# Strassen's seven quarter products for the output projection of a hybrid gMLP and attention layer

## The chip, the cores and the metric

The kernel runs on one core of a Trainium2 chip. The metric is the device time of one execution in microseconds (us), the median of the runs of one program. TensorE is written PE, VectorE DVE, ScalarE ACT, GpSimd POOL; SP is the queue that issues most DMAs.

## What is computed

One layer of a diffusion trunk with 1024 latent tokens and 128 context tokens of width 1024, all in 32-bit floats. A gMLP group and an attention group of four heads each give 512 columns per token; they are gated, put side by side and projected:

```python
def _back(x, gate, a_out, attn, g_b, w_o):
    y = jnp.concatenate([a_out, attn * jax.nn.silu(g_b)], axis=-1) @ w_o
    return x + gate * y
...
y_prompt = _rmsnorm(xp, final_g)
y_sample = _rmsnorm(xs, final_g)
```

`w_o` is 1024 x 1024. The change touches this product and what follows it.

## The kernel before

Tokens are cut into nine tiles of 128: tiles 0 to 7 are latent, tile 8 is context. After the input projections the gated gMLP output stands in `mixA`, the attention output in `mixB`, both 128 x 4 x 1152: four chunks of 128 mix columns, then tokens. So `mixA` is the upper half of the projection's inner dimension (chunks k = 0 to 3), `mixB` the lower (k = 4 to 7).

A product of 32-bit accuracy is made of three passes. Each operand is split into a high part of type float32r and a low part, operand minus high part (`lo_of`, L111, on DVE); the passes are high x high, high x low, low x high (`out_terms`, L1793).

The order on every engine is written out by hand: from L1774 on, `manual_schedule` keeps the instructions of PE, ACT, DVE and POOL in the order in which Python records them, and SP's queue is ordered as well. Python keeps a clock of its own (`now`): `run` (L207) records a step and moves the clock by its cost, `later(dt, fn)` (L167) records `fn` when the clock passes now + dt, `merged` (L212) interleaves two lists of steps. An instruction that must wait therefore holds up all that was recorded behind it on its engine.

The attention goes through 32 heads (8 tiles x 4). Scores, maximum (L1478), exponentials (L1488), the scaling of the 128 x 1280 exponentials by POOL (`divide`, L1491), then transposes on PE (L1550), the split of the transposed values into `ph` (ACT, L1554) and `pl` (DVE, L112), and the products with the values (L1574 to L1576), two heads at a time. `closed` and `opened` end and begin pools of SBUF; a tile of a new pool waits for the last users of what lay there.

Beside it, from head 11 on, the rows of `w_o` are loaded (`wo_piece`, L1630) and split by `split_job` (L1608): high part by POOL, low part by DVE, one job after each `divide`. `his` and `los` are the lists of such jobs; `wo_need` (L1660) records what is missing before a matmul uses it. The split pieces of `w_o` fill the SBUF areas that the attention no longer uses (`flat`, and the key tiles `kch`, `kcl`, `krh`, `krl`). Tiles 8 and 0 are split in the same way; 20 of their steps are interleaved with the last heads (`early`, L1840).

After the last head the rest follows tile by tile: 8 and 0, then 1 to 7 (L1916 to L1935). A tile takes 2 halves x 8 chunks x 3 passes = 48 matmuls of 512 columns; the last one has its second half in two quarters (`LASTP`). Splits of the next tile: two ACT copies and two DVE low parts. `finish` (L1865) multiplies a half out of PSUM by the gate, adds the residual row `xr`, lets ACT square it with a running sum, and then scales the row by the inverse root (Newton's steps on DVE) and the norm's weight `fg`. `finish_last` (L1881) does the same for tile 7 in a shorter chain, with POOL preparing the weighted row `z` and the store cut over two queues.

The gates come from DRAM (`gdram`), spread over all partitions.

Of the kernel before, what the change touches and what calls it, by code (L numbers as in the profile page):

```python
# [14 lines left out]
ALU = mybir.AluOpType  # L15
# [79 lines left out]
def tile_hymba_step(ctx: ExitStack, tc: tile.TileContext, I, O):  # L95
# [156 lines left out]
    gdram = gd.tile([4, 512], F32, tag="gdram", name="gdram")  # L252
    scl = pc.tile([P, NT], F32, tag="scl", name="scl")
# [1211 lines left out]
    es = {}  # L1465
    s2 = pss.tile([P, 2, 256], F32, tag="s2", name="s2", bufs=1)

    def softmax(t, h, lat_, con_):
# [305 lines left out]
    with tc.manual_schedule(engines=engines):  # L1774
# [3 lines left out]
        def mix_tiles(t):  # L1778
            mh[t] = flat[0][4 + len(mh) % 2].rearrange("p (c q) -> p c q", c=8)
            ml[t] = wo.tile([P, 8, P], F32R, tag="ml", name=f"ml{t}", bufs=2)  # L1780
            sl = slice(t * P, (t + 1) * P)
            return [(mh[t][:, 4 * i : 4 * i + 4, :], ml[t][:, 4 * i : 4 * i + 4, :], src[:, :, sl]) for i, src in enumerate((mixA, mixB))]

        def mix_split(t):
            for hi, lo, src in mix_tiles(t):
                S.copy(hi, src)
                lo_of(lo, src, hi)

        def mix_jobs(t):
            for i, (hi, lo, src) in enumerate(mix_tiles(t)):  # L1790
                split_job(lambda hi=hi, src=src: pool_copy(hi, src), lambda hi=hi, lo=lo, src=src: lo_of(lo, src, hi), ("m", t, i))
# [12 lines left out]
        for c in range(len(pairs)):  # L1804
# [11 lines left out]
            if 2 * c + LEAD + 1 == 11:  # L1816
                closed(c_ra)
                c_wo, wo = opened("wo", side="left")
                for k in range(2):
                    wo_piece(k, *flat[0][2 * k : 2 * k + 2])  # L1820
                mix_jobs(8)
                mix_jobs(0)
# [10 lines left out]
        for t in (8, 0):  # L1833
            wps[t] = [psw.tile([P, 512], F32, tag="w", name=f"w{t}{i}") for i in range(2)]

        def load_xr(t):
# [3 lines left out]
        early = [  # L1840
            (0.65, lambda t=t, i=i, k=k: out_terms(t, wps[t][i], 512 * i, 512 * i + 512, [k]))
            for k in range(5) for t in (8, 0) for i in range(2)
        ]
# [10 lines left out]
    for t in (8, 0, 1, 2):  # L1854
        load_xr(t)
# [3 lines left out]
    gate = {}  # L1859

    for cond in (1, 0):
        gate[cond] = ep.tile([P, 4, 256], F32, tag=f"gate{cond}", name=f"gate{cond}")
        nc.sync.dma_start(gate[cond], gdram.rearrange("j (c r) -> c j r", c=2)[cond : cond + 1].broadcast_to([P, 4, 256]))

    def finish(t, parts):  # L1865
        y = ep.tile([P, 1024], F32, tag="y", name=f"y{t}", bufs=2)
        gt = gate[0 if t < NS else 1].rearrange("p j r -> p (j r)")
        n = len(parts)
        ss = sm.tile([P, 4], F32, tag="fss", name=f"fss{t}")
        for j, (ps, c0, c1) in enumerate(parts):  # L1870
            V.tensor_tensor(y[:, c0:c1], ps, gt[:, c0:c1], op=ALU.mult)
            V.tensor_tensor(y[:, c0:c1], y[:, c0:c1], xr[t][:, c0:c1], op=ALU.add)
            S.activation(xr[t][:, c0:c1], y[:, c0:c1], AF.Square, accum_out=ss[:, j : j + 1])
        s1 = sm.tile([P, 1], F32, tag="fs1", name=f"fs1{t}")
        V.tensor_reduce(s1, ss[:, :n], axis=AX.X, op=ALU.add)
        v = mean_eps(sm, s1, 1, 1024.0, "f")
        r = rsqrt(sm, v, 1, "f")
        V.scalar_tensor_tensor(y, y, r, fg, op0=ALU.mult, op1=ALU.mult)
        nc.sync.dma_start(O["y"][t], y)

    def finish_last(t, parts):  # L1881

        y = ep.tile([P, 1024], F32, tag="y", name=f"y{t}", bufs=2)
        z = ep.tile([P, 1024], F32, tag="xr", name=f"z{t}", bufs=4)
        gt = gate[0].rearrange("p j r -> p (j r)")
        ss = sm.tile([P, 4], F32, tag="fss", name=f"fss{t}")
# [3 lines left out]
        n = len(parts)  # L1890
        for j, (ps, c0, c1) in enumerate(parts):
            V.tensor_tensor(y[:, c0:c1], ps, gt[:, c0:c1], op=ALU.mult)
            V.tensor_tensor(y[:, c0:c1], y[:, c0:c1], xr[t][:, c0:c1], op=ALU.add)
            if j < n - 1:
                S.activation(xr[t][:, c0:c1], y[:, c0:c1], AF.Square, accum_out=ss[:, j : j + 1])
            else:
                V.scalar_tensor_tensor(junk[:, : c1 - c0], y[:, c0:c1], 1.0, y[:, c0:c1], op0=ALU.mult, op1=ALU.mult, accum_out=ss[:, j : j + 1])
            G.tensor_tensor(z[:, c0:c1], y[:, c0:c1], fg[:, c0:c1], op=ALU.mult)
            if j == n - 2:
                V.tensor_reduce(v0, ss[:, : n - 1], axis=AX.X, op=ALU.add)  # L1900
                V.tensor_scalar(v0, v0, 1.0 / 1024.0, EPS, op0=ALU.mult, op1=ALU.add)
# [128 lines left out]
```

## Time and profile before

| | |
|---|---|
| Runs, us | 621.58, 621.84, 623.27; median 621.84 |
| Span of the profiled execution, first to last instruction | 620.5 us (its time as a run is not listed) |
| Mean granted PE clock | 0.991 |
| After the last attention matmul (528.4 to 613.0) | 396 matmuls |
| HBM read and written in the whole execution | 40.87 MB and 4.83 MB |

The span begins with the first instruction of any engine and ends with the last; a run's time has some start and end around it. Busy time of PE says how long matmuls were in flight, and these overlap; PEld is the loading of weights into the array. The chain of waits follows the last instruction back to what released it, step by step. In a group's line stand: source line, engine, operation, tiles written and read with their shapes, count, then busy time in us and mean ns of one, then the idle time of the engine just before and what ended it. In a timeline line: start, length, engine, line, operation; "x2" means that two were merged into one line.

### The profile page before, as it was taken

The page shows a single profiled execution, that of the slowest core. Times are in us where ns is not written, and L with a number is a line of the kernel's source. Part 1 is how long each engine was busy: PE and PEld are TensorE (multiplying, and loading weights), DVE is VectorE, ACT ScalarE, POOL GpSimd, SP SyncE. Part 2 cuts the span into 40 slices and gives each one's busy share as a digit, 9 for nine tenths or more (in the row PEclk, how much of TensorE's full clock was granted, in tenths as well). Part 3 has the DMA queues.
Part 4 walks back from the last instruction along what each step waited for, and adds up shares of the span by engine and source line. Part 5 has one row for each costly group of instructions (what it writes and reads, how often), then busy time and mean ns, then how long its engine had stood idle before and what let it go on. Part 6 is the DMA issues. An engine that isn't in the chain of part 4 may idle for free.

```text
span 620.5 us, 9955 instructions
## 1 busy us (share of the span) xinstructions
PE 606.8 (98%) x3719; PEld 549.0 (88%) x3719; DVE 411.3 (66%) x938; ACT 298.9 (48%) x694; POOL 123.2 (20%) x167
## 2 busy tenths in 40 slices
PE   7999999999999999999999999999999999999995
PEld 6777889999989999999998899999999988888884
DVE  4685457997756468566778656767666754577655
ACT  6556764345433245455675565555555632232212
POOL 2461112000000000433364112323222241000001
PEclk8999999999999999999999999999999999999998
DMA  8992010100351133100010000000101113423311
GB/s 316 393 380 71 0 35 2 35 0 3 134 208 70 64 106 122 38 1 1 1 42 1 1 2 0 2 9 27 35 1 35 35 68 129 144 101 137 115 55 68
DMA packets 15327, 46.32 MB, mean 75 GB/s; under 512 B 1824, under 2 KB 4784, under 8 KB 14768
## 3 DMA queue, kind: packets, MB, share of 16 engines
q1 hardware_dynamic: 15136, 45.50, 20.7%
q8 instruction: 29, 0.48, 0.3%
q10 hardware_dynamic: 144, 0.20, 0.1%
q14 instruction: 18, 0.15, 0.1%
HBM read 40.87 MB, written 4.83 MB: 74 GB/s over the span
## 4 chain that ended last, share of the span: by engine, by line
PE 93%; DVE 3%; DMA 1%; ACT 1%; issue 1%; SPq 0%; ACTq 0%
PE p L953 10%; PE tp L751 8%; PE tp L975 5%; PE pT L1550 5%; PE w L1797 5%; PE w L1799 5%; PE w L1798 5%; PE s L1505 3%; PE s L1506 3%; PE s L1504 3%; PE s L1503 3%; PE o L1574 3%; PE s L1507 3%; PE o L1576 3%; PE o L1575 3%; PE zacc L1389 2%
## 5 line engine op out<-in xcount | busy, mean ns | idle before, releaser
L112 DVE TENSOR_TENSOR pl<-pT,ph 128x512 fp32r<-128x512 f32 x81 | 55.4, 687 | 48.8 <-ACT ph L1554 48.2
L1488 ACT ACTIVATE e<-s,nb,scl 128x256 f32<-128x256 f32 x64 | 56.1, 881 | 35.1 <-DVE nb L1482 35.1
L1494 POOL TENSOR_SCALAR e<-e,rs 128x1280 f32<-128x1280 f32 x32 | 43.0, 1343 | 130.2 <-DVE rs L1493 124.7
L1554 ACT CAST ph<-pT 128x512 fp32r<-128x512 f32 x80 | 45.5, 588 | 41.9 <-PE pT L1550 39.0
L751 PE MATMUL tp<-area,w 128*128 128x384 f32 x288 | 52.5, 338 | 0.0
L751 PEld LDWEIGHTS tp<-area,w 128*128 128x128 f32 x288 | 50.4, 188 | 0.4
L1550 PE MATMUL pT<-ident,e 128*128 128x128 f32 x320 | 48.0, 272 | 1.3 <-DVE pl L112 1.2
L1574 PE MATMUL o<-ph,vh 128*128 128x256 f32 x160 | 47.8, 299 | 0.0
L1576 PE MATMUL o<-ph,vl 128*128 128x256 f32 x160 | 44.9, 281 | 0.0
L1575 PE MATMUL o<-pl,vh 128*128 128x256 f32 x160 | 44.7, 280 | 0.0
L1799 PE MATMUL w<-area,ml 128*128 128x512 f32 (+1 forms) x114 | 43.2, 379 | 0.0
L1550 PEld LDWEIGHTS pT<-ident,e 128*128 128x128 f32 x320 | 37.4, 140 | 4.8 <-issue 1.6
L1478 DVE TENSOR_REDUCE m<-s 128x1 f32<-128x1024 f32 x32 | 38.9, 1217 | 1.5 <-PE s L1507 1.5
L1503 PE MATMUL s<-kch,area 128*128 128x512 f32 (+2 forms) x100 | 38.9, 389 | 0.0
L1236 POOL TENSOR_TENSOR kr<-z,rope 128x64 f32<-128x64 f32 x8 | 2.6, 321 | 172.0 <-ACT z L1245 172.0
L1506 PE MATMUL s<-krh,area 128*128 128x512 f32 (+2 forms) x100 | 35.4, 354 | 0.0
L1505 PE MATMUL s<-kch,area 128*128 128x512 f32 (+2 forms) x100 | 35.4, 354 | 0.0
L1504 PE MATMUL s<-kcl,area 128*128 128x512 f32 (+2 forms) x100 | 35.3, 353 | 0.0
L1507 PE MATMUL s<-krl,area 128*128 128x512 f32 (+2 forms) x100 | 35.1, 351 | 0.0
L975 PE MATMUL tp<-area,w 128*128 128x384 f32 x192 | 35.0, 337 | 0.0
L975 PEld LDWEIGHTS tp<-area,w 128*128 128x128 f32 x192 | 33.6, 188 | 0.4 <-issue 0.4
L1574 PEld LDWEIGHTS o<-ph,vh 128*128 128x128 f32 x160 | 30.1, 188 | 1.6
(375 smaller groups left out, 1601.1 us busy)
## 6 DMA issues: line engine op xcount, KB each, us to landing
ada<-in_ada_ss SPq DMA_DIRECT2D x16, 512.0 KB, 8.1
w2r<-in_w_t SPq DMA_DIRECT2D x12, 512.0 KB, 4.4
x<-in_x SPq DMA_DIRECT2D x9, 512.0 KB, 7.4
xr<-in_x SPq DMA_DIRECT2D x9, 512.0 KB, 4.0
adag<-in_ada_g SPq DMA_DIRECT2D x4, 1024.0 KB, 4.8
wor<-in_w_o SPq DMA_DIRECT2D x8, 512.0 KB, 3.4
out_y<-y SPq DMA_DIRECT2D x8, 512.0 KB, 4.8
wvr<-in_w_v SPq DMA_DIRECT2D x8, 256.0 KB, 9.2
```

What stands on the lines that cost most here:

```text
L112: V.tensor_tensor(lo, src, f32(hi), op=ALU.subtract)
L751: T.matmul(tps[i, g][:, :GW], w_[i][:, k, :], x_[k, g], start=k == 0 and j == 0, stop=k == NK - 1 and j == 2)
L953: T.matmul(banks[key], a_, b_, start=k == 0 and m == 0, stop=k == 3 and m == len(passes) - 1)
L975: T.matmul(tps[c, 2][:, :GW], w_[c][:, k, :], x_[k, 2], start=k == 0 and m == 0, stop=k == NK - 1 and m == 2)
L1488: S.activation(e[:, sl], src, AF.Exp, bias=nb, scale=scl[:, t : t + 1], accum_out=su[:, i : i + 1])
L1503: T.matmul(ps, qh_, kch[:, sl], start=True, stop=False)
L1505: T.matmul(ps, ql_, kch[:, sl], start=False, stop=False)
L1550: T.transpose(ps[:, w : w + P], es[t, h][:, c * P : (c + 1) * P], ident)
L1574: T.matmul(o, vh[:, kt, :], ph[:, sl], start=c == 0, stop=False)
L1575: T.matmul(o, vh[:, kt, :], pl[:, sl], start=False, stop=False)
L1576: T.matmul(o, vl[:, kt, :], ph[:, sl], start=False, stop=c == n - 1)
L1799: T.matmul(ps, b, woh[k][:, c0:c1], start=False, stop=k == NK - 1)
```

## The change

Tiles 0 to 7 are taken in four pairs (a, b). The four quarters of the left side are A11 = `mixA` of a, A12 = `mixB` of a, A21 = `mixA` of b, A22 = `mixB` of b; those of `w_o` are B11, B12, B21, B22 (rows 0 to 511 or 512 to 1023, columns 0 to 511 or 512 to 1023). With

S1 = A21 + A22, S2 = S1 - A11, S3 = A11 - A21, S4 = A12 - S2, T1 = B12 - B11, T2 = B22 - T1, T3 = B22 - B12, T4 = B21 - T2,

seven products of 128 x 512 by 512 x 512 (12 matmuls each: 4 chunks x 3 passes) stand in place of eight: A11 B11, A12 B21, S4 B22, S2 T2, S1 T1, S3 T3, A22 T4. Tile 8 keeps the plain product.

- **Weight sums.** After head 5 a pool `tp` is open. In eight units (chunk k, half of the columns) SP loads four 128 x 256 blocks of `w_o`, POOL makes the four sums, ACT the high parts, DVE the low parts, and SP stores both in DRAM (`tdram`). A unit starts after a `divide`, once per head. Loading and splitting `w_o` itself begins at head 15 instead of 11, with up to two jobs after a `divide`.
- **Fetching them.** Near the end of the attention POOL's queue fetches T2 (4 DMAs) and T3 (8), after it T1 and T4 (8), 4 MB in all of T1 and T4. The gates and the rows of x follow on SP's queue.
- **Block sums** S1 to S4: four POOL operations per pair, made one pair ahead.
- **Splits of the left blocks** into a ring of five buffers, four products ahead (`split`): ACT writes the high part and a copy of the block in PSUM, DVE takes the low part from there.
- **Sums of the products.** K (in A11's place), W (A12's), C (S2's) collect them: DVE adds out of PSUM, POOL multiplies by the gate and adds to the residual row. ACT squares into a buffer that is free. The inverse root is one ACT root with one Newton step.
- **The last pair** has the order A11, A12, S2, S1, S4, S3, A22, and its last product is made and finished in two quarters of 256 columns.

The core of the diff:

```diff
-            spare_hi(1)
-            spare_lo(1)
+            spare_hi(2 if len(his) > 2 else 1)
+            spare_lo(2 if len(los) > 2 else 1)
+            if units and units[0] in traw:
+                unit_of[0](units.pop(0))
...
+        def t_unit(u):
+            k, c = divmod(u, 2)
+            raw = traw[u]
+            b11, b12, b21, b22 = (raw[:, i, :] for i in range(4))
+            sub(G, b11, b12, b11)
+            sub(G, b12, b22, b12)
+            sub(G, b22, b22, b11)
+            sub(G, b21, b21, b22)
+            hi = tp.tile([P, 4, 256], F32R, tag="hi", name=f"thi{u}")
...
+            for i in range(2):
+                later(3.2 + 1.5 * i, lambda i=i: high(i))
+                later(4.0 + 1.5 * i, lambda i=i: low(i))
...
+        def t_piece(m, k, piece):
+            th[m, k], tl[m, k] = piece[:, 0:512], piece[:, 512:1024]
+            G.dma_start(piece, tdram[m - 1, k].rearrange("p s c -> p (s c)"))
...
+        def product(q, ps, c0=0, c1=512, ks=range(4)):
...
+            need(("blk", q))
+            blk = ring(q)
+            for k in ks:
+                bh, bl = right(queue[q][2], k)
+                three(ps[:, c0:c1], (blk[:, 0, k, :], blk[:, 1, k, :]), (bh[:, c0:c1], bl[:, c0:c1]), k == 0, k == 3)
...
+    for n, (m, k) in enumerate([(1, k) for k in range(4)] + [(4, k) for k in range(4)]):
+        t_piece(m, k, tpiece[n])
+        if n == 3:
+            load_gate(0, tag="gate0")
+    load_gate(1, tag="xr", bufs=4)
+    load_xr(8)
+    load_xr(0)
+    load_xr(1)
...
+        def high():
+            cell["raw"] = pso.tile([P, 512], F32, tag="o", name=f"raw{q}").rearrange("p (k c) -> p k c", k=4)
+            S.copy(ring(q)[:, 0], block(n, name))
+            S.copy(cell["raw"], block(n, name))
...
+        def low():
+            lo_of(ring(q)[:, 1], cell["raw"], ring(q)[:, 0])
+            made.add(("blk", q))
...
+            if name == "A11":
+                later(dt, lambda: S.copy(K, view(ps)))
+            elif name == "A12":
+                later(dt, lambda: add(V, view(ps), view(ps), K))
+                later(dt + 0.7, lambda: V.tensor_tensor(C, view(ps), gL, op=ALU.mult))
+                plus(C, a, L, dt + 1.4, 0)
+            elif name == "S2":
+                later(dt, lambda: add(V, K, view(ps), K))
...
+            elif name == "S4" and last:
+                later(dt, lambda: add(V, view(ps), view(ps), W))
+                in_place(a, R, ps, dt + 0.05, 1)
+                gated_add(W, gR, b, R, dt + 0.1)
+                norm(a, dt + 2.0)
...
+                else:
+                    later(dt, lambda: V.tensor_tensor(W, view(ps), gR, op=ALU.mult))
+                    later(dt + 0.2, lambda: V.tensor_tensor(half(b, R), half(b, R), W, op=ALU.add))
+                    later(dt + 0.4, lambda: V.tensor_tensor(ps, ps, gate[0][:, L], op=ALU.mult))
+                    later(dt + 0.6, lambda: V.tensor_tensor(xr[b][:, L], ps, xr[b][:, L], op=ALU.add))
...
+    spare_hi(len(his))
+    for i, c in enumerate((L, R)):
+        in_place(8, c, wps[8][i], 6.5 + 1.4 * i, i)
+    norm(8, 12.0)
+    for n in range(3):
+        pair(n)
+    zl = ep.tile([P, 1024], F32, tag="xr", name="zl", bufs=4)
+    pair(3)
```

`in_place(t, c, ps, ...)` is gate product and residual sum on DVE and the square on ACT, as before but with the product left in PSUM. `norm` is the scaling of a whole row. `finish_last` keeps its chain, with two parts instead of three.

More of the change, by code (lines that the diff above doesn't have):

```diff
@@ L1776, in tile_hymba_step @@
         tail = []
[L1778 to L1787, printed above, removed]
@@ new lines, in need_lo, with t_load @@
+        def need_lo(key):
+            while key not in made:
+                if los:
+                    spare_lo(1)
+                else:
+                    now_, (due, fn) = now[0], waiting.pop(0)
+                    now[0] = due
+                    fn()
+                    now[0] = now_
+        th, tl = {}, {}
+        def t_load(u):
+            k, c = divmod(u, 2)
+            raw = traw[u] = tp.tile([P, 4, 256], F32, tag="raw", name=f"traw{u}", bufs=2)
+            for i, row in enumerate((k, k + 4)):
+                nc.sync.dma_start(raw[:, 2 * i : 2 * i + 2, :], I["w_o"][row].rearrange("p (s c) -> p s c", s=2)[:, :, 256 * c : 256 * c + 256])
@@ L1865, in finish @@
[L1865 to L1886, printed above, removed]
+    ssq = {}
+    def square_of(t, j, junk, c0, c1):
+        if t not in ssq:
+            ssq[t] = sm.tile([P, 4], F32, tag="fss", name=f"fss{t}", bufs=3)
+        S.activation(junk, xr[t][:, c0:c1], AF.Square, accum_out=ssq[t][:, j : j + 1])
@@ new lines, in split @@
+    def split(q, dt):
+        if q >= len(queue):
+            return
+        n, name, _ = queue[q]
+        cell = {}
+        def high():
[5 more added lines that the diff above has]
+            made.add(("blk", q))
+        later(dt, high)
+        later(dt + 1.3, low)
```

296 lines of the change are left out of this document (247 added, 49 removed).

## The prediction

> **What bounds the kernel now.** I read the page first (busy time, then the chain that ended last), then the windows of the stages which the change touches, then the matmuls one by one. The page says that TensorE (PE) is busy nearly all the time and carries the chain.
>
> ```profile
> span 620.5 us, 9955 instructions
> PE 606.8 (98%) x3719; PEld 549.0 (88%) x3719; DVE 411.3 (66%) x938; ACT 298.9 (48%) x694; POOL 123.2 (20%) x167
> ...
> PE 93%; DVE 3%; DMA 1%; ACT 1%; issue 1%; SPq 0%; ACTq 0%
> ```
>
> The windows say the same of both stages, and how much room the others have. Columns: length, then busy time (count) of PE, PE's weight loads, DVE, ACT, POOL, then clock, DMA share, GB/s.
>
> ```profile
> 528.40:613.00 84.60, 84.60 (x396) 70.86 (x395) 55.31 (x149) 20.92 (x49) 2.04 (x2) 1.00 0.30 104
> 360.00:366.00 6.00, 6.00 (x45) 5.56 (x44) 4.63 (x10) 3.39 (x7) 2.56 (x2) 1.00 0.00 0
> 366.00:372.00 6.00, 6.00 (x45) 5.53 (x43) 3.01 (x8) 3.40 (x7) 0.12 (x1) 1.00 0.02 4
> 528.00:532.00 4.00, 4.00 (x21) 3.33 (x20) 0.42 (x1) 0.00 (x0) 0.00 (x0) 1.00 0.93 308
> 36.00:40.00 4.00, 4.00 (x33) 2.88 (x33) 3.86 (x9) 0.35 (x3) 2.36 (x3) 1.00 1.02 400
> ```
>
> From 528.4 to 613.0, the output projection after the attention, PE never rests, POOL has next to nothing and DVE a third free. So there a matmul that is left out is worth its whole pitch, as long as the others keep up. Busy time of a matmul is no pitch (they overlap); the pitch is read from starts:
>
> ```profile
> 575.20 0.39 PE L1797 MATMUL w<-area 128*128 128x512 f32 x1
> ...
> 601.04 0.39 PE L1797 MATMUL w<-area,area 128*128 128x512 f32 x1
> ...
> 607.16 0.28 PE L1797 MATMUL w<-area 128*128 128x256 f32 x1
> ...
> 612.56 0.28 PE L1797 MATMUL w<-area,area 128*128 128x256 f32 x1
> ```
>
> Between the first two starts lie 114 matmuls: 25.84 / 114 = 0.2267 us for 512 columns. Between the last two lie 45: 0.120 us for 256. Test: 348 x 0.2267 + 48 x 0.120 = 84.6, the window.
>
> **Matmuls: -11.0 us.** Tiles 0 to 7 take 8 x 8 x 2 x 3 = 384 passes of 512 columns, the last 24 of them as 48 of 256. Four pairs of seven products take 4 x 7 x 4 x 3 = 336, the last 12 as 24 of 256. What follows the attention falls from 84.6 to 312 x 0.2267 + 24 x 0.120 = 73.6 us. The order of the built programs has these 60 rows fewer on PE, so that the change does not leave them out is excluded.
>
> **What a pair adds beside its 84 x 0.2267 = 19.0 us of PE.** The prices:
>
> ```profile
> L1872 DVE TENSOR_TENSOR y<-y,xr 128x512 f32<-128x512 f32 x16 | 10.8, 687 | 0.2
> L1878 DVE SCALAR_TENSOR_TENSOR y<-y,fr,fg 128x1024 f32<-128x1024 f32 x8 | 10.3, 1285 | 0.2
> L1786 ACT CAST area<-mixB 128x512 fp32r<-128x512 f32 x7 | 4.4, 622 | 16.0 <-PE w L1798 16.0
> L1873 ACT ACTIVATE xr<-y 128x512 f32<-128x512 f32 x16 | 10.1, 630 | 39.5 <-DVE y L1872 20.0 <-issue 19.3 <-DVE ft L122 0.2
> L1211 ACT ACTIVATE zw<-ssz,epsb 128x1 f32<-128x1 f32 x18 | 4.2, 286 | 0.0
> L1898 POOL TENSOR_TENSOR z<-y,fg 128x512 f32<-128x512 f32 x1 | 1.3, 1296 | 92.9 <-DVE y L1893 92.9
> L1310 POOL TENSOR_TENSOR qr<-qr,qr 128x256 f32<-128x256 f32 x8 | 5.9, 734 | 0.6
> ```
>
> DVE: 7 low parts and 8 sums out of PSUM at 0.69, two row scalings at 1.29 with five one-column steps of about 0.2: at most 14.9 us. POOL: 4 sums of blocks, 3 gate products, 4 adds at 1.30: 14.3. ACT: 14 copies at 0.62, one copy, 4 squares of 0.75 with their read (next fence), 2 roots: 12.9. Copies into PSUM and DVE operations in place in PSUM are not in the trace; I take the rows of the same shape. All stay below 19.0, and a split is made four products (10.9 us) ahead, so within pairs 1 and 2 I cost it at nothing. That cover is thin: POOL slower by a third is 19.0.
>
> **The end: +4.2 us.** Here it does not hide. DVE works in its written order, and between the fifth product of the last pair and the last half-product it has a long row of work: three operations on tile 6's right half, wait for ACT's square, the one-column steps with ACT's root, four operations on tile 7, the scaling of tile 6, and only then the first half of the last product.
>
> ```profile
> 601.92 0.69 DVE L1871 TENSOR_TENSOR y<-w,gate 128x512 f32<-128x512 f32 x1 [3.48 <-PE w L1799]
> 602.65 0.69 DVE L1872 TENSOR_TENSOR y<-y,xr 128x512 f32<-128x512 f32 x1
> 603.38 0.63 ACT L1873 ACTIVATE xr<-y 128x512 f32<-128x512 f32 x1 [4.12 <-DVE y L1872]
> 604.13 0.15 DVE L1875 TENSOR_REDUCE fs<-fss 128x1 f32<-128x2 f32 x1 [0.79 <-ACT xr L1873]
> 607.44 0.68 DVE L1892 TENSOR_TENSOR y<-w,gate 128x512 f32<-128x512 f32 x1
> 610.24 0.42 DVE L1892 TENSOR_TENSOR y<-w,gate 128x256 f32<-128x256 f32 x1 [1.38 <-PE w L1799]
> 610.70 0.43 DVE L1893 TENSOR_TENSOR y<-y,xr 128x256 f32<-128x256 f32 x1
> ```
>
> A dependent 512 step costs 0.73, a 256 step 0.46, an ACT square up to the next DVE step 0.75; DVE starts 0.28 after the next product's first matmul (607.16 to 607.44). Let E be PE's end. The fifth product is done at E - 2.88 - 2.72 = E - 5.60; DVE begins at E - 5.32; three steps: E - 3.16; square: E - 2.4; sum, root (0.29), reciprocal with their hand-overs, about 0.75: E - 1.65. Four 512 operations with three small ones between, 2.9: E + 1.3. Scaling, 1.2 to the next start: E + 2.5. First half, 0.46 + 0.46, its square about 0.55, two small steps 0.4: E + 4.35. Only there begins what today begins 0.19 after E:
>
> ```profile
> 613.11 0.43 DVE y L1892
> ```
>
> From 613.11 to the end, 7.4 us, the operations stay the same. So 4.35 - 0.19 = 4.2 us late. Bounds: 3.0, if the hand-overs cost nothing and independent steps run at 0.6; 5.5, if POOL's work stretches DVE's.
>
> **After the attention: +1.6 us.**
>
> ```profile
> 527.93 0.47 PE at L1593 x4
> ```
>
> ```profile
> 514.60 1.63 POOL L115 TENSOR_SCALAR area<-wor 128x512 fp32r<-128x512 f32 x2 [6.91 <-DMA wor<-in_w_o]
> 527.25 0.33 SPq L1857 DMA_DIRECT2D fg<-in_final_g  x1
> 527.62 0.99 SPq L1863 DMA_DIRECT2D gate<-gdram  x2
> ```
>
> Let t = 0 be 527.93. In place of 3.5 MB, SP loads 3 MB here (gates, three x rows, the norm's row) and POOL fetches T1 and T4, 4 MB, on a queue of its own. Ahead of and with x row 0 SP moves 2 MB; with POOL's queue sharing a rate between 308 and 400 GB/s, say 380, that is 10.5 us: it lands at t + 9.8. Behind it stand in line POOL's first add (1.30) and ACT's square of tile 0 (0.75), and behind that on ACT the square of tile 8 (0.63), which frees the PSUM bank of pair 0's sixth product: with hand-overs of 0.4, t + 12.9. PE reaches that product at 0.45 + 48 x 0.2267 = t + 11.3. So 1.6 us; 0 if SP's queue has the rate to itself (landing at t + 4.8), 4.1 at a shared 308 GB/s. POOL's four sums for pair 1 then end near t + 17, its third product is due at t + 22: covered. DVE's chain runs late in pair 0, and regains some 4 us per pair.
>
> What one of POOL's DMAs costs POOL, c, no row shows. Below: SP's 0.33; above: POOL's 1.30 for a sum, and beyond it rival 3; I take 0.5, since a DMA's own row is nearest (the gates' two issues took 0.99). T1's last piece is the 16th behind the first copy at 514.60: 516.8 + 16c, 4.0 to land (row below), needed at t + 0.45 + 45 x 0.2267 = 538.6: in time up to c = 1.1.
>
> ```profile
> xr<-in_x SPq DMA_DIRECT2D x9, 512.0 KB, 4.0
> ```
>
> [...]
>
> **In the attention: +1.0 us.** Eight units of weight sums, one per head, each with four POOL sums (0.73), two ACT copies (0.62), two DVE low parts (0.69), ten SP DMAs. Two heads take 12.0 us of PE with 7.64 of DVE, 6.79 of ACT, 2.7 of POOL. With two units: 10.4, 9.3 and 8.6. So PE stays the bound, and only a late low part can stop it. The shortest distance:
>
> ```profile
> 358.92 0.69 DVE L112 TENSOR_TENSOR pl<-pT,ph 128x512 fp32r<-128x512 f32 x1 [2.45 <-ACT ph L1554]
> 361.24 0.28 PE L1574 MATMUL o<-ph,vh 128*128 128x256 f32 x1
> 505.65 0.98 DVE L112 TENSOR_TENSOR area<-wor,area 128x512 fp32r<-128x512 f32 x1
> 506.06 1.64 POOL L115 TENSOR_SCALAR krh<-wor 128x512 fp32r<-128x512 f32 x2
> ```
>
> The low part is ready at 359.6, 1.6 us before its use, and a unit puts a copy and a low part ahead of it: 1.3. That leaves 0.3, less where the exponentials start later behind the unit's first copy. I take 1.0 once, not per head; bounds 0 and, if DVE saturates, 5.6 (below). The sums' DMAs are small beside an idle DMA system (0.00 to 0.02).
>
> **Sum** against the profiled span of 620.5: -11.0 + 4.2 + 1.6 + 1.0 = -4.2, so 616.3. The median of the runs, 621.84, lies 1.34 above the span; that stays: **617.6 us**.
>
> **Rivals.** (1) All but the end hides, and the end costs 3.0: 621.84 - 11.0 + 3.0 = 613.8. For it: idle DMA and POOL; against: the x row is queued as written. (2) DVE becomes the bound while the units run. In the last fence a DVE low part with both inputs in SBUF took 0.98 and POOL's two copies beside it 1.64, for 0.69 and twice 0.62 elsewhere. If each of four low parts waits for one POOL sum, DVE needs 10.4 + 4 x 0.73 = 13.4 per 12.0 us; over four such periods 5.6, in place of 1.0: 622.2. [...] (3) Slower: POOL's DMAs hold POOL. T4's last piece is issued at 516.8 + 20c, lands 4.0 later, and is needed at t + 0.45 + 69 x 0.2267 = 544.0: PE waits 20c - 23.2, in place of 1.6. From c = 1.45 the gain is gone; at c = 2.0 it is 16.8, so 632.8. For it: 20 in a row on one queue, never seen here; against: POOL is otherwise idle then.
>
> **How the numbers follow.** Forecast, 615 to 620: 0.42. Rival 1: 0.25. Rival 2: 0.17. Rival 3: 0.13; the rest is spread. Measurement tells 0.3%, 1.9 us, from no change: faster below 619.97 takes the forecast, rival 1 and little more, 0.67; within, most of rival 2, 0.18; slower 0.15. The range of 8 in 10 takes in rival 1's neighbourhood down to 612.5 and rival 2's up to 624.0, and leaves out most of rival 3 and the case of 610.8 in which nothing is paid.
>
> **What would show it.** Matmul pitch 0.227 and 336 rows after the attention; DVE's first step on the last half-product some 4 us after PE's last matmul, without idle time before it; a gap on PE at pair 0's sixth product, released by ACT; PE still at 6.00 of 6.00 between 345 and 395; POOL's DMAs at under 1 us. It is wrong if PE shows gaps inside pairs 1 to 3 (splits late), if T1 or T4 release PE, or if DVE idles at the end.

## The result and the profile after

The changed kernel takes 644.49 us (median of four runs, 642.50 to 645.48); the kernel before takes 621.71 beside it. The ratio is 1.036, with an interval of 1.033 to 1.038. The forecast was 617.6, with a range up to 624.0: wrong in sign and outside the range.

The page of the profiled execution: span, busy time, chain.

```profile
span 643.7 us, 10209 instructions
PE 605.0 (94%) x3659; PEld 543.6 (84%) x3659; DVE 435.8 (68%) x931; ACT 328.6 (51%) x758; POOL 215.4 (33%) x262
...
DVE 1%; ACT 0%; issue 0%; ACTq 0%
```

PE has the 60 matmuls less, yet its busy time fell by only 1.8 us, and the chain that ended last could be followed back for 10 us only, mostly on DVE. Where the 23.2 us of span come from is read from three marks that both traces have: the last attention matmul on PE, the last matmul, and the end.

```profile
527.76 0.63 PE L1593 MATMUL at<-os,wuv 128*128 128x128 f32 x4
...
612.80 0.28 PE L1799 MATMUL w<-area,ml 128*128 128x256 f32 x1
```

That was the kernel before, in the timeline of PE; this is the changed one.

```profile
541.90 0.64 PE L1597 MATMUL at<-os,wuv 128*128 128x128 f32 x4
...
625.46 0.28 PE L1904 MATMUL A<-vlt,ringC 128*128 128x256 f32 x1
```

| | before | after | difference | forecast |
|---|---|---|---|---|
| to the last attention matmul | 527.8 | 541.9 | +14.1 | +1.0 |
| from there to the last matmul | 85.0 | 83.6 | -1.5 | -11.0 + 1.6 |
| from there to the end of the span | 7.7 | 18.2 | +10.5 | +4.2 |

**In the attention** the kernel before had PE at 6.00 of 6.00. Windows of the changed kernel while the weight sums run, in the columns of the prediction:

```profile
372.00:378.00 6.00, 4.37 (x34) 3.95 (x33) 4.39 (x9) 2.60 (x7) 2.08 (x2) 1.00 0.36 112
378.00:384.00 6.00, 3.98 (x22) 3.56 (x21) 2.17 (x6) 3.73 (x8) 2.97 (x4) 0.83 0.56 188
...
390.00:396.00 6.00, 3.97 (x20) 3.75 (x19) 4.83 (x9) 2.63 (x7) 3.26 (x4) 0.72 0.81 257
...
414.00:420.00 6.00, 6.00 (x46) 5.56 (x45) 3.11 (x5) 2.89 (x7) 1.34 (x1) 1.00 0.01 3
```

No engine is full here, not DVE either (2.2 to 4.8 of 6). PE stands still, and in some windows the clock is low as well. One stop, followed through the timelines of POOL, ACT, DVE and PE (the bracket holds the idle time before and what ended it):

```profile
387.93 0.62 ACT L1876 CAST thi<-traw 128x512 fp32r<-128x512 f32 x1 [3.81 <-POOL traw L809]
388.45 0.56 ACT L1490 ACTIVATE e<-s,nb,scl 128x256 f32<-128x256 f32 x1
...
390.69 1.07 ACT L1558 CAST ph<-pT 128x512 fp32r<-128x512 f32 x2
...
391.44 0.68 DVE L112 TENSOR_TENSOR pl<-pT,ph 128x512 fp32r<-128x512 f32 x1
...
392.18 1.09 PE L1554 MATMUL pT<-ident,e 128*128 128x128 f32 x4 [2.03 <-DVE rs L1494]
```

ACT's copy of a unit's sums waits 3.81 us for POOL. Behind it in ACT's order stand the exponentials, behind them the splits of the transposed values, behind these DVE's low part, and behind that PE. (PE's line names `rs`, but that step ends at 392.19, after PE has begun; the low part ends at 392.12.)

**After the attention** the DMA system is full (share 1.10, 395 GB/s in the next fence), and T4 is late; then the clock is at half.

```profile
541.90:560.00 18.10, 15.62 (x71) 12.68 (x70) 8.15 (x13) 5.60 (x10) 2.92 (x6) 0.99 1.10 395
560.00:565.00 5.00, 3.94 (x8) 2.65 (x9) 1.92 (x4) 2.99 (x8) 4.92 (x5) 0.50 0.23 90
```

```profile
560.23 0.79 PE L1902 MATMUL A<-vht,ringB 128*128 128x512 f32 x1 [2.70 <-DMA vht<-tdram]
...
582.83 0.50 PE L1904 MATMUL A<-tp,area 128*128 128x512 f32 x1 [0.66 <-DVE area L112]
...
602.82 0.50 PE L1904 MATMUL A<-tp,area 128*128 128x512 f32 x1 [0.63 <-DVE area L112]
```

The last two are the third matmul of one pair's last product and of the next pair's: a pair takes 19.99 us and not 84 x 0.2267 = 19.04, and each time a low part of DVE is late.

**At the end** the last matmul ends near E = 625.58. DVE's timeline:

```profile
612.08 0.49 DVE L2048 TENSOR_TENSOR fs<-fss 128x1 f32<-128x1 f32 x1 [1.66 <-ACT mixB L2036]
...
613.97 1.22 DVE L2061 SCALAR_TENSOR_TENSOR fw<-fw,fv 128x1 f32<-128x1 f32 x1
...
624.28 0.70 DVE L806 TENSOR_TENSOR S<-S,mixB 128x512 f32<-128x512 f32 x1
...
629.48 0.69 DVE L2143 TENSOR_TENSOR mixB<-S,gate 128x512 f32<-128x512 f32 x1 [0.83 <-POOL xr L2110]
...
634.03 0.42 DVE L2200 TENSOR_TENSOR A<-A,gate 128x256 f32<-128x256 f32 x1
...
635.83 0.42 DVE L2200 TENSOR_TENSOR A<-A,gate 128x256 f32<-128x256 f32 x1
```

DVE begins on the fifth product of the last pair (L806, 624.28) at E - 1.3, where the forecast had E - 5.32. The two halves of the last product follow at E + 8.5 and E + 10.3, forecast E + 2.5 and E + 4.35.

### The profile page after: what moved, and what is told of

Its sections match the earlier page's. It is cut to its first block, busy times and chain, and to the rows that moved or that the text cites. A ratio compares the mean times of both kernels' runs of the same rounds, so it can differ in the third digit from the quotient of the medians.

```text
span 643.7 us, 10209 instructions
## 1 busy us (share of the span) xinstructions
PE 605.0 (94%) x3659; PEld 543.6 (84%) x3659; DVE 435.8 (68%) x931; ACT 328.6 (51%) x758; POOL 215.4 (33%) x262
## 5 line engine op out<-in xcount | busy, mean ns | idle before, releaser
L1496 POOL TENSOR_SCALAR e<-e,rs 128x1280 f32<-128x1280 f32 x32 | 45.1, 1409 | 108.7 <-DVE rs L1495 88.2
L1554 PE MATMUL pT<-ident,e 128*128 128x128 f32 x320 | 49.3, 277 | 9.2 <-DVE rs L1494 4.1
L1579 PEld LDWEIGHTS o<-pl,vh 128*128 128x128 f32 x160 | 31.1, 194 | 1.4
```

Source lines behind the costliest of these rows:

```text
L1554: T.transpose(ps[:, w : w + P], es[t, h][:, c * P : (c + 1) * P], ident)
L1579: T.matmul(o, vh[:, kt, :], pl[:, sl], start=False, stop=False)
```

## Experiments

All runs are told against the same three marks. "Behind" is the last attention matmul against 527.76 of the kernel before, "PE" the time from there to the last matmul, "tail" from the last matmul to ACT's last scaling (3.5 us in the kernel before, 13.6 in the changed one). The first mark scatters: it was 14.1, 11.0, 13.0, 11.9, 10.1, 11.5 and 10.7 behind in the seven profiled executions that have the attention of the changed kernel (itself, early T2 and T3, rows, scale, late norm, early sums, no norm). Some of that stands before the first unit: at 340 us the runs lie between 1.6 us ahead of the kernel before and 0.5 behind. Where a loss per unit is given, it is therefore counted from there to the matmuls behind the eighth unit. The column "PE" scatters too: the twelve executions that change nothing behind the attention took 82.8 to 85.2.

| run | time, us | ratio (interval) | behind | PE | tail |
|---|---|---|---|---|---|
| changed kernel | 644.49 | 1.036 (1.033-1.038) | 14.1 | 83.6 | 13.6 |
| one store | 642.79 | 1.034 (1.028-1.039) | 10.2 | 83.2 | 13.6 |
| no traffic | 638.52 | 1.027 (1.024-1.030) | 6.4 | 83.5 | 13.6 |
| no arithmetic | 632.06 | 1.017 (1.014-1.020) | 0.4 | 83.6 | 13.6 |
| early T2, T3 | 641.96 | 1.033 (1.030-1.036) | 11.0 | 82.5 | 13.6 |
| shift | 644.50 | 1.038 (1.034-1.043) | 11.1 | 84.5 | 13.6 |
| shift, one store | 643.58 | 1.037 (1.032-1.041) | 12.1 | 84.5 | 13.6 |
| rows | 640.80 | 1.032 (1.029-1.036) | 13.0 | 80.4 | 13.6 |
| scale | 644.45 | 1.038 (1.035-1.041) | 11.9 | 84.3 | 13.6 |
| no traffic, shift | 641.17 | 1.031 (1.027-1.035) | 8.4 | 85.2 | 13.6 |
| spread | 643.27 | 1.034 (1.030-1.038) | 11.7 | 84.3 | 13.6 |
| late norm | 643.50 | 1.035 (1.031-1.038) | 10.1 | 86.2 | 13.1 |
| all | 646.21 | 1.040 (1.037-1.043) | 14.5 | 82.6 | 13.1 |
| slots | 650.43 | 1.047 (1.041-1.052) | 19.2 | 83.2 | 13.6 |
| no low parts | 632.13 | 1.017 (1.011-1.024) | 1.0 | 84.4 | 13.6 |
| no copies | 640.90 | 1.031 (1.026-1.036) | 9.3 | 83.0 | 13.9 |
| early sums | 645.25 | 1.038 (1.033-1.044) | 11.5 | 86.5 | 13.5 |
| slots, other head | 645.01 | 1.037 (1.034-1.040) | 14.7 | 82.8 | 13.6 |
| no norm | 632.63 | 1.017 (1.014-1.020) | 10.7 | 79.3 | 8.1 |

### The attention: transfers or engines

Theory Q was that SP's queue is too slow for the units, theory D that the engines have too much to do.

**One store:** `store` writes four blocks with one DMA, in a layout of `tdram` with the block first.

```diff
-                for m, j in ((1, 0), (3, 1), (4, 2), (2, 3)):
-                    nc.sync.dma_start(f32(tdram[m - 1, k][:, i, ...]), src[:, j, :])
+                nc.sync.dma_start(f32(tdram[:, k, :, i, ...]).rearrange("j p c -> p j c"), src)
```

> Same work as the changed kernel; each unit of weight sums is stored with two DMAs (512 KB each) in place of eight of 128 KB. Theory Q (SP's queue is the bound of the units: load 1.2 us of issue, eight stores 4.1, then about 2.3 until the store has landed before the next load of the same buffer may start, 7.65 per unit against 6.0 per head; ACT's copies of late sums hold the exponentials behind them): SP's turn per unit falls to about 5.0, PE is no longer stopped between 370 and 412, the last attention matmul comes 0 to 3 us behind that of the kernel before in place of 14.0, time about 632. Rival D (DVE, ACT and POOL have too much to do in their written order, whatever the loads): still 10 or more behind, time about 644.

**No traffic** and **no arithmetic:**

```diff
-            raw = traw[u]
+            raw = traw[u % 2]
...
-                    store(0, f32(hi))
-                    store(1, raw)
-                    if u + 2 < 8:
-                        t_load(u + 2)
```

> The units' arithmetic is kept, on two buffers loaded once; the stores and the later loads are left out (T is fetched from rows of the weight that are put there before the attention, so the projection's result is not the reference's). Theory Q: the last attention matmul 0 to 3 us behind the kernel before, time about 632. Rival D: 10 or more behind, time about 644. A third, C (the units' DMA traffic itself disturbs PE or the engines): as Q here.

```diff
-            sub(G, b11, b12, b11)
...
-                S.copy(hi[...], raw[...])
-                lo_of(raw[...].bitcast(F32R), raw[...], hi[...])
```

> All loads and stores of the units are kept, their sums, copies and low parts are left out (the stores carry the raw blocks, so the projection's result is not the reference's). Theory Q: loads come as late as before, but nothing on ACT, DVE or POOL waits for them: 0 to 1 us behind, time about 630. Rival D: the same. Rival C: 10 or more behind, about 644.

Measured: 10.2, 6.4 and 0.4 behind. Theory Q falls as the whole cause: eight stores or two make no difference clear of the scatter, and without any transfer 6.4 remain. Theory C, the traffic itself, falls too: with all transfers and no arithmetic PE never rests.

```profile
372.00:384.00 12.00, 12.00 (x86) 11.08 (x85) 7.59 (x17) 6.74 (x15) 2.65 (x3) 1.00 0.85 262
```

So the arithmetic is needed for the loss, and late loads add 4 to 8 us to it.

### The attention: when the operations stand

**Shift**, alone, with one store, and without traffic: the copies and low parts 2.2 us later.

```diff
-                later(3.2 + 1.5 * i, lambda i=i: high(i))
-                later(4.0 + 1.5 * i, lambda i=i: low(i))
+                later(5.4 + 1.5 * i, lambda i=i: high(i))
+                later(6.2 + 1.5 * i, lambda i=i: low(i))
```

> The changed kernel with one number altered: ACT's copies and DVE's low parts of a unit are written 2.2 us later behind the scaling of the exponentials (5.4, 6.9 and 6.2, 7.7 in place of 3.2, 4.7 and 4.0, 5.5). Theory O (order: POOL's four sums end 5.0 us after the scaling starts, so that a copy written at 3.2 waits for them and holds back the exponentials, the splits of the transposed values and with them PE): ACT's waits for the sums (13.6 us in all) fall below 3, the last attention matmul comes at most 4 us behind the kernel before in place of 11 to 14, time about 634. Theory O with SP's loop of 7.65 us per unit as a second bound: 6 to 8 us behind, about 638. Rival D (DVE, ACT and POOL have too much work, in any order): 10 or more behind, about 643.

> Both: copies and low parts 2.2 us later, and two stores per unit in place of eight. Theory O, with or without SP's loop: 0 to 3 us behind, time about 632. Rival D: 10 or more behind, about 643.

> As the run without traffic (stores and later loads of the units left out, T not the reference's), with copies and low parts 2.2 us later. Without the shift that run was 6.3 us behind. Theory L (two loops: one of order, POOL's scaling, two sums, ACT's copy, the exponentials behind it, DVE's reciprocal, POOL's next scaling; one of the two raw buffers, each held about 13 us from load to stored low part, 15 with the shift, for 12 us of two heads; the shift opens the first and tightens the second): with the second loop gone as well, 0 to 2 us behind, time about 633. Rival D (amount of work on DVE, ACT and POOL): still 5 or more behind, about 638.

Measured: 11.1, 12.1 and 8.4 behind. ACT's wait for the sums did go (13.6 to 0.2 us), but nothing was gained: theory O, and theory L after it, had seen a real wait that was not the only one. The timeline of the third run, DVE and then PE, shows the next:

```profile
380.24 1.34 DVE L112 TENSOR_TENSOR traw<-traw,thi 128x512 fp32r<-128x512 f32 x1
381.50 1.21 DVE L1483 TENSOR_REDUCE m<-s 128x1 f32<-128x1024 f32 x1
382.64 0.90 DVE L112 TENSOR_TENSOR traw<-traw,thi 128x512 fp32r<-128x512 f32 x1
...
384.51 0.45 DVE L1487 SCALAR_TENSOR_TENSOR nb<-m,nscl 128x1 f32<-128x1 f32 x1
...
388.09 0.65 PE L1557 MATMUL pT<-ident,e 128*128 128x128 f32 x4 [1.23 <-DVE pl L112]
```

Two low parts of a unit (`traw`), 0.69 us each by themselves and 1.34 and 0.90 beside POOL's sums, stand ahead of and between a head's two maxima. They delay the shift (`nb`), ACT waits for it (3.45 us here), and with the exponentials everything behind them.

**Spread:** with shift and one store, the units at eight of 14 heads.

```diff
-            if units and units[0] in traw:
-                unit_of[0](units.pop(0))
+            if unit_of:
+                turn[0] += 1
+                if units and turn[0] in (0, 2, 3, 5, 7, 8, 10, 12):
+                    unit_of[0](units.pop(0))
```

> Shift of 2.2 us, two stores per unit, and the eight units spread over 14 heads (the loads of the weight begin at head 19 in place of 15), so that a raw buffer has 20 us. All work is done. Theory L: 0 to 3 us behind, time about 634. Rival D: the same work costs the same, 8 or more behind, 640 or more.

Measured: 8.5 us were lost over the eight units (from 0.5 to 9.0 behind), 1.1 per unit, about as many as before. A unit costs by itself, not by crowding; theory L falls.

**No low parts** and **no copies**, both on the run without traffic with the shift: the line `lo_of(raw...)` is left out, or the line `S.copy(hi...)` (the low parts then read the sums in place of the high parts).

> The run without traffic and with the shift (8.4 us behind), and without DVE's low parts; sums and copies are kept (T not the reference's). Theory S: 0 to 1.5 us behind at the last attention matmul. Rival U (ACT's copies stand ahead of the splits of the transposed values): 5 or more. Rival T, as far as POOL's sums also lengthen DVE's other steps: 2 to 4.

> The same run with DVE's operations kept (they take the sums themselves in place of the high parts) and without ACT's copies. Theory S: 6 to 9 us behind. Rival U: 0 to 2.

Measured: 1.0 and 9.3 behind, where both together gave 8.4. DVE's low parts cost it, ACT's copies do not (in this place of theirs).

**Slots:** one store; one unit per two heads; copies ahead of the shift of a head, low parts right behind it.

```diff
+            job = pend.pop(0) if h % 2 == 0 and pend else None
+            if job:
+                job[0](0)
+                job[0](1)
             V.tensor_reduce(m[:, 1:2], con_, axis=AX.X, op=ALU.max)
             V.scalar_tensor_tensor(nb, m[:, 0:1], m[:, 1:2], nscl[:, t : t + 1], op0=ALU.max, op1=ALU.mult)
+            if job:
+                job[1](0)
+                job[1](1)
```

> All work is done, two stores per unit; one unit per two heads, its sums after the scaling of an even head, its two copies on ACT right ahead of the next even head's exponentials (idle there 1.44 us in the kernel before), its two low parts on DVE right behind that head's shift (idle there 2.45 us). The weight itself is loaded from head 23, so that late splits may stop PE behind that; read is the place of the attention matmul behind the last unit. Theory S (DVE's low parts between a head's two maxima delay its shift, by it the exponentials, by them the split of the next transposed values in ACT's order, and PE): at most 0.25 us per unit, 2 us behind in all, where the spread run was 9.0 behind after its eight units. Rival T (POOL's sums beside two-input operations of DVE lengthen both, wherever they stand): 0.8 us or more per unit, 6 or more behind.

Measured: 0.8 us per unit (6.5 for eight, from 1.6 ahead to 4.9 behind), what rival T had named. But DVE's timeline shows why:

```profile
399.01 0.22 DVE L1488 SCALAR_TENSOR_TENSOR nb<-m,nscl 128x1 f32<-128x1 f32 x1
399.19 1.29 DVE L112 TENSOR_TENSOR traw<-traw,thi 128x512 fp32r<-128x512 f32 x2
400.40 0.68 DVE L112 TENSOR_TENSOR pl<-pT,ph 128x512 fp32r<-128x512 f32 x1
```

In this head the low part `pl`, for which PE waits, follows the shift at once; the idle 2.39 us are in the other head. The same with `h % 2 == 1`:

> As the run with the slots, with the other head of each two: sums after the scaling of an odd head, copies ahead of the next odd head's exponentials, low parts behind its shift, where DVE is idle for 2.39 us. All work is done. Theory S (a low part costs what it delays, and nothing where DVE is idle): 0.2 us or less per unit, 0 to 2 us behind after the eighth unit, where that run was 4.9 and the spread run 9.0 behind. Rival T (POOL's sums and DVE's low parts lengthen each other wherever they stand): 0.8 us per unit again. The weight is loaded from head 23 here too, so the end of the attention is late and the time is not read.

```profile
404.61 0.22 DVE L1488 SCALAR_TENSOR_TENSOR nb<-m,nscl 128x1 f32<-128x1 f32 x1
404.79 1.29 DVE L112 TENSOR_TENSOR traw<-traw,thi 128x512 fp32r<-128x512 f32 x2
407.22 0.69 DVE L112 TENSOR_TENSOR pl<-pT,ph 128x512 fp32r<-128x512 f32 x1 [1.14 <-ACT ph L1565]
```

Measured: 0.5 us were lost over the eight units (from 0.1 to 0.6 behind), 0.06 per unit, with all sums, copies, low parts, loads and stores done; the run without arithmetic drifts by as much over this stretch. Theory S holds, and theory D falls: the same amount of work costs 8.5, 6.5 or 0.5 us by where it stands. The runs without low parts and without copies say that it is DVE's low parts; for ACT's copies in the unshifted kernel that is argued from the stop shown above, and no run shows it. What follows these units in both slot runs is not theirs: the weight itself is loaded from head 23 only, POOL's splits wait for it, and in the run with the other head PE loses 13.6 us there, mostly by stops of 1.7 and 6.7 us and the clock at half for 10 us around them.

### After the attention

**Early T2, T3** and **rows** (which has both):

```diff
-            if k == 4 and i == 1:
+            if k == 0 and i == 1:
                 for n in range(4):
                     t_piece(2, n, flat[2][2 + n])
-            if k == 6 and i == 1:
+            if k == 4 and i == 1:
...
-    load_gate(1, tag="xr", bufs=4)
-    load_xr(8)
-    load_xr(0)
-    load_xr(1)
+    nc.sync.dma_start(xr[0], I["x"][0])
...
+    nc.sync.dma_start(xr[8], I["x"][8])
...
+    G.dma_start(xr[1], I["x"][1])
...
-    nc.sync.dma_start(fg, I["final_g"].broadcast_to([P, 1024]))
+    G.dma_start(fg, I["final_g"].broadcast_to([P, 1024]))
```

> Only the place of two fetches changes: T2 is fetched five steps earlier in the drain of the attention, T3 two chunks earlier, so that 4 MB are moved before the last 4 MB of T1 and T4. Theory B (from 530 to 560 the DMA system is full, 372 to 404 GB/s, and T4 is late for its place in that line): the last piece of T4 lands at least 4 us earlier against the last attention matmul, PE's waits of 2.7 and 0.8 us for vht and vlt go, the clock stays at 1.0 behind them, and 4 to 6 us are gained: about 639. Rival (T4's last pieces wait for the buffers of the values, vh and vl, that the attention frees last): no change, about 644.5.

> Only the place of transfers changes: T2 and T3 earlier (as in the run before), x row 0 ahead of the second gate and of x row 8 on SP's queue, x row 1 and the norm's row behind T4 on POOL's queue. Theory B (a full DMA system after the attention; x row 0, late by it, holds POOL's sum, behind it ACT's square and behind that ACT's splits, 9.2 to 9.4 us): ACT's wait falls to 4 us or less, PE's waits for T4, for the bank of tile 8 and for the first low parts go, and from the last attention matmul to the last matmul it takes 79 to 80 us in place of 83.6 and 82.5. Rival (DVE is behind anyway in pair 0, by its own row of work): 82 or more.

Measured: 82.5 and 80.4 us of PE. In the first the wait for `vht` went, one of 0.78 for `vlt` stayed, and the next were PE's waits for the bank of tile 8 (1.07) and for DVE's low parts (1.46): most of the gain went into a new wait. In the second no transfer stops PE directly any more. The 82.5 is hardly clear of the scatter of 82.8 to 85.2; the 80.4 is. Theory B holds for T4; ACT's wait, though, only changed its source, since now tile 8 is the late one:

```profile
ACT w L2042 <- DVE xr L2096: 8.1, 1, 8.1
...
DVE w L2095 <- DMA gate<-gdram: 5.4, 1, 5.4
```

### The pairs and the end

**Scale:** rows 1, 3 and 5 are multiplied by the norm's weight on POOL and scaled on ACT. **Late norm:** `norm(a, dt + 5.6)` becomes `norm(a, dt + 10.5)`. **Early sums:** the first three of `s_sums(n + 1)` at product 1 in place of 3, for n = 1 and 2.

```diff
+            if t in (1, 3, 5):
+                G.tensor_tensor(xr[t], xr[t], fg, op=ALU.mult)
...
+                S.activation(xr[t], xr[t], AF.Copy, scale=cell["fr"])
```

> The scaling of rows 1, 3 and 5 is taken from DVE (1.28 us each): POOL multiplies by the norm's weight, ACT scales by the inverse root. Theory E (DVE works behind the products by about 4 us from pair 2 on, because its written row waits for squares which wait for POOL, and the two scalings stand in that row; the end then shows the whole lag): the last matmul to the end falls from 18.1 to 15.5 us, PE's waits of 0.66 and 0.90 for late low parts go, and from the last attention matmul to the last matmul it takes about 1.5 us less. Rival (POOL's row of gate products and sums, 1.30 each, sets the end, and gets 2.6 us more per pair here): the end stays at 18 or grows.

> The changed kernel with the norm of each pair's first row written 4.9 us later, behind that of the second row. Theory X (the row of DVE waits 1.66 us for the square of that row, which waits for POOL, and its one-column steps, 0.15 us by themselves, take 0.43 to 1.22 beside a POOL operation): that wait and those lengths go, PE's waits of 0.66 and 0.90 for low parts shrink, from the last attention matmul to the last matmul it takes 1 to 2 us less than 83.6, and from the last matmul to the last scaling on ACT 11.5 in place of 13.6. Rival (the row is only put in another order, POOL's sums set the end): 13.5 as before.

> The changed kernel; in pairs 1 and 2 three of the four block sums for the next pair are written two products earlier, where POOL stands idle for 5.7 us (596.5 to 602.2 in the changed kernel). Theory P (POOL's row, 13 us without a break from the first block sum to the last gated sum, makes the squares late, these hold ACT's splits and DVE's row): POOL's gated sums start 3 to 4 us earlier, DVE's wait of 1.66 goes, PE's waits of 0.63 and 0.90 for low parts go, from the last attention matmul to the last matmul it takes 1.5 us less than 83.6, and from the last matmul to ACT's last scaling 10.5 in place of 13.6. Rival (DVE's own row): 13 or more, and 83 or more.

Measured: tails of 13.6, 13.1 and 13.5, and PE 84.3, 86.2 and 86.5. None helped: 84.3 is within the scatter, the other two are above it, and all three made PE wait longer for a low part (1.28, 3.33 and 2.24 us in place of 0.66). Theories E, X and P fall as they were put. In the first, one step took from DVE comes back as a wait. POOL, then DVE:

```profile
615.88 2.57 POOL L2052 TENSOR_TENSOR xr<-xr,fg 128x1024 f32<-128x1024 f32 x1 [1.08 <-ACT mixA L2036]
```

```profile
616.72 1.75 DVE L2048 TENSOR_TENSOR fs<-fss 128x1 f32<-128x1 f32 x1
```

The one-column sum, 0.15 us elsewhere, ends with POOL's instruction.

**No norm:** for tiles 0 to 5 `norm` only stores the row.

```diff
+        if t < 6:
+            later(dt + 1.45, lambda: (nc.sync.dma_start(O["y"][t], xr[t]), made.add(("y", t))))
+            return
```

> The changed kernel without the norms of rows 0 to 5: the inverse roots and the scalings are left out and the rows stored without them (squares are still made); tiles 6 to 8 as before. Theory R (DVE's written row, about 16 us of work and 4 us of waits per pair, is the bound in the pairs, and its lag of 4 us stands at the end): PE's waits of 0.66, 0.63 and 0.90 go, a pair takes 19.1 us in place of 20.0, DVE begins with the fifth product of the last pair 1 us or less behind its end in place of 4, and from the last matmul to ACT's last scaling it takes 9 to 10 us in place of 13.6. Rival P (POOL's row is the bound): 13 or more and 20.0.

Measured: PE 79.3, tail 8.1, and a pair takes 19.04 us (577.45 to 596.49, third matmul of the last product to that of the next pair). PE waits for no low part from pair 1 on. DVE's first steps on the fifth product and on the first half:

```profile
612.56 0.70 DVE L806 TENSOR_TENSOR S<-S,mixB 128x512 f32<-128x512 f32 x1 [2.03 <-PE S L1904]
...
621.02 0.42 DVE L2203 TENSOR_TENSOR A<-A,gate 128x256 f32<-128x256 f32 x1
```

Here E is 617.95, and DVE now waits for PE: theory R holds. POOL's row is unchanged and does not stand in the way. The run leaves out DVE's steps, their waits and ACT's roots together, so it does not say which of these weighs most.

**All** (spread, shift, one store, rows, late norm):

> All together: the spread units with shift and two stores, the transfers after the attention in the order of the run with the rows, and the late norm. By theories L, B and X 8 to 10, 3 and 3 us less than the changed kernel, about 629; it is no faster than the kernel before unless the pairs lose their waits too.

Measured: 646.21, no better than the changed kernel. The units lost 8.5 us (from 1.1 ahead to 7.4 behind), the weight's splits, begun at head 19, another 6.5 (a wait of 4.76 on PE, and the clock at half behind it), and with the late norm PE waits 3.36 at one low part.

No run beat the kernel before. From measured parts a bound can be estimated: units at no cost (+0.5), the transfers as in the rows run (80.4 - 85.0 = -4.6) and the end as it is (+10.5) give 6.4 us more than before; with PE and end of the run without norms (-5.7 and +5.1) it would be even. Both are bounds that no run reached: the +0.5 for the units was seen only together with the late start of the weight, which cost 13.6.

## Why the prediction was wrong

**Matmuls, -11.0: right.** The pitch is 0.2267, and where nothing stops PE a pair takes 19.04 us.

**"In the attention: +1.0 ... I take 1.0 once, not per head": the step that failed most.** It cost 10.1 to 14.1. Putting "a copy and a low part" ahead of the needed low part, 1.3 us of its 1.6, left out two things. The copy itself waits: in the stop shown ACT stood 3.81 us for POOL's sums, 13.6 over all units. And the unit's low parts delay more than the one low part: in the run without traffic with the shift 1.34 and 0.90 us of them stand ahead of a head's `nb`, and ACT's exponentials wait 3.45 for it. Then the loss was taken once. PE has no idle time (6.00 of 6.00 before the change) from which a late head could be made up, so each of the eight units pays again, 1.1 us in the spread run. The place decides the cost: 0.06 per unit in DVE's idle stretch of the right head. "The sums' DMAs are small beside an idle DMA system" was right for the traffic alone (0.4 behind) and wrong together with the sums: loads that come late lengthen each stop. Rival 2 named DVE, and the low parts do lengthen beside POOL's sums (1.34 and 0.90 for 0.69), but it had DVE as an engine that fills up (5.6 us); it was at 4.8 of 6 or less in the windows shown.

**"Inside pairs 1 and 2 I cost it at nothing": wrong by 1.0 us per pair.** DVE's work was somewhat more than priced (15.4 to 15.9 per pair, at most 14.9 forecast), but it was compared with 19.0 as a sum. In DVE's written order the waits count as well (for ACT's squares, raw copies and roots, in turn behind POOL), and the sum of work and waits is the pair's 20.0.

**"The end: +4.2": the chain right, its start wrong.** With DVE in time, in the run without norms, the fifth product was taken up at E - 5.39 (forecast - 5.32), the halves at E + 3.1 and + 4.9 (+ 2.5 and + 4.35), and the end came 5.1 later than before, within the bounds. The step that failed is "DVE's chain runs late in pair 0, and regains some 4 us per pair": it regains nothing, since its row of work and waits is as long as the pair. In the changed kernel it starts 4.0 late, and POOL's late sum (0.83) and one-column steps beside POOL make most of 1.9 more.

**"After the attention: +1.6": wrong place, too small.** c was right (0.53 to 0.58 per DMA, so rival 3 did not come about as put). The gap came at T4 and not at the sixth product. The step that failed is the landing of x row 0 at t + 9.8, and with it the 4.0 us for T4 to land: POOL's wait for row 0 ended at 559.39, t + 17.3 (t is 542.07 here). The rate, 395 GB/s, was within the bounds taken, but 4 MB had been put ahead of and with row 0, and nothing ahead of T4. In the 18.1 us from the last attention matmul to 560 the queues moved 7.1 MB (18.1 x 0.395), about all that both had to bring after the attention, and T4 was in that line too; its piece `vht` took 16.2:

```profile
vht<-tdram POOLq DMA_DIRECT2D x1, 512.0 KB, 16.2
```

PE stood still for 2.70 and 0.84 us there. Behind the first of these the clock was at 0.50 until about 566.4 (0.50 from 560 to 565, a mean of 0.96 from 565 to 582), and for that the prediction had no term.

**The sum:** 616.3 forecast and 643.7 measured for the span; the 27.4 between them are 13.1 in the attention, 7.9 from there to the last matmul, 6.3 at the end.

What stays open: how much of the unshifted kernel's loss is ACT's copies and how much DVE's low parts, since only with the shift each was taken away alone. Whether the units can stand in their cheap place and the weight still come in time is open too: no run has both.

## What to carry to other kernels

Where the order on each engine is fixed and the bound engine has no idle time, an added operation costs what it delays, every time it occurs, and its busy time says nothing of that (here 8.5, 6.5 or 0.5 us for the same eight units): look for the stretch in which its engine waits, per head or per pair, and put it there. Compare an engine's work and its waits together with the period, not its busy share. Before a stage is started, add up all bytes in all queues that must land in it, and give every one the time of the sum (here 7.1 MB in 18.1 us, of which the 0.5 MB of `vht` took 16.2).

## What the runs showed of the hardware

A stop of PE could cost a second time here, by the clock. Windows of 2 us of the changed kernel: a stop of PE of 2.02 us, then the clock at half for 2 us and, by the mean of 0.65, for 1.4 us more, and then full again.

```profile
380.00:382.00 2.00, 0.04 (x1) 0.00 (x0) 1.02 (x2) 1.73 (x4) 0.98 (x2) 1.00 0.30 98
382.00:384.00 2.00, 1.95 (x9) 1.95 (x10) 1.15 (x4) 2.00 (x5) 0.78 (x1) 0.50 0.33 106
384.00:386.00 2.00, 2.00 (x11) 1.91 (x10) 2.00 (x3) 0.11 (x1) 1.76 (x2) 0.65 0.93 284
386.00:388.00 2.00, 2.00 (x16) 1.82 (x16) 0.95 (x3) 0.07 (x1) 1.61 (x3) 1.00 1.03 354
```

In the run without traffic the stops are shorter, 1.65 us at most, and the clock stays at 1.00 there:

```profile
386.00:388.00 2.00, 0.35 (x4) 0.14 (x2) 1.36 (x3) 1.83 (x5) 0.00 (x0) 1.00 0.00 0
388.00:390.00 2.00, 2.00 (x16) 1.97 (x17) 1.99 (x4) 0.58 (x1) 1.63 (x2) 1.00 0.00 0
```

So the stop of 2.02 us cost an estimated 1.7 us more by the clock (half of 3.4). The length alone does not decide it: in the run with one store a stop of 1.83 us (388.90 to 390.73) was followed by 0.54 and 0.61 in the windows from 392 to 396, and in the run with the early sums one of 3.25 us (386.82 to 390.07) left the clock at 1.00 up to 396. Nor is the clock what makes the loss: the changed kernel has three such stretches beside the units, an estimated 5.1 of its 14.1 us, and the run with the shift has 1.00 from 340 to 541 and is 11.1 behind all the same.

The norm's one-column DVE steps with two inputs (L2048, L2060 to L2062) that began while a POOL instruction ran ended here only with it: they took 0.15 to 0.16 us alone, 1.22 beside POOL in the changed kernel (613.97 to 615.19, POOL's product 613.88 to 615.17) and 1.75 in the run with the scale (616.72 to 618.47, POOL's product to 618.45). The reciprocal (L2059), with one input, took 0.16 beside POOL too (613.31 to 613.47, POOL's sum 612.63 to 613.92). The prediction had only one longer operation to go by, a low part of 0.98 us for 0.69.
